# A decoder block with a product-key expert mixer: more buffers for expert rows, fewer for gathered rows, and another pacing of lookups and gathered rows beside the dense expert passes

## The chip, the cores and the metric

The kernel runs on one core of one Trainium2 chip. The metric is the device time of one execution in microseconds. Three runs of the kernel before took 1950.27, 1951.07 and 1956.48 us; the median is 1951.07 us.

## What is computed

A token block of 512 rows (plus 16 meta tokens) of width 1024 goes through an attention and gated-linear-attention mixer and then through a mixer of 16384 single-neuron experts. For the change only the second part matters, cut here to its core:

```python
s1, s2 = scores of each head's query halves against 128 keys each
v1, i1 = top_k(s1, 16);  v2, i2 = top_k(s2, 16)
sc, pos = top_k(v1[:, None] + v2[None, :], 16)          # 8 heads x 16 experts per token
eidx  = take(i1 * 128 + i2, pos);  gates = softmax(sc)
act   = gelu(einsum('nkd,nd->nk', expert_u[eidx], x))   # U
y     = einsum('nk,nkd->nd', gates * act, expert_v[eidx])  # V
```

Everything is float32; products on TensorE are made of three float32r products of a high and a low part (`mm3`).

## The kernel before, in words

The 512 tokens are four blocks of 128. For blocks 0 to 2 (`DENSE`) the mixer is dense: every one of the 128 groups of 128 experts is multiplied with all 384 tokens. The pass over U, `u_phase(i1)` for 128 values of i1, loads a 512 KB block `uf` of U on SP's queue (L960), splits it into `uh` on ScalarE (L185) and `ul` on VectorE (L186), makes 24 matmuls into a bank `pj`, and writes the gelu `ge`; the first 24 results stay in SBUF, the others go to DRAM (`Ad`) in pairs of blocks on ScalarE's queue. The pass over V, `v_operands(i1)` and `v_block`, again for 128 values, loads a 512 KB block of V into the same tiles `uf` (L1006), reads `ge` back from `Ad` (L1003, one load for two blocks), multiplies it with the gates `gt` (L1021), splits both and makes 18 matmuls of 512 columns into six accumulators. `gt` comes from a table `Gd` in DRAM, 1.5 MB for eight blocks in rows of 512 bytes, also on SP's queue (L1019), two buffers.

`Gd` is written beforehand: for each dense token block `topk` finds the experts (VectorE alone but for 32 matmuls) and `spread` turns them into gate tables by one-hot products: `B` on VectorE (L877), `Am` on GpSimd (L879), matmuls into banks `px` and `pk` (L883), a copy `st` on ScalarE (L884), 32 such pieces a block.

For token block 3 (`GATHER`) the mixer is sparse: `gathered(3)` fetches for each of its 128 choices the 128 rows of U (`u_dot`, a 512 KB indirect DMA from GpSimd's queue into `gu`, L823, and a dot product on VectorE, L830) and later the 128 rows of V (`v_sum`, the same DMA and a multiply-add into `y` on VectorE, L841): 256 gathered tiles in all, called rows below, into a ring of `GB` buffers.

What mixes these is a queue of Python generators. After each block i1 the kernel calls `look.run(4.3 * RATES[0])` while lookups and spreads are left, then `rows.run(4.3 * RATES[0])` for gathered rows beside U, and `rows.run(4.3 * RATES[1])` beside V. Each generator yields a guess of its cost in us (a lookup piece 1.4, a spread piece 1.0, a row 1.3), and `run` takes pieces until the budget is spent. The gathered rows can't start before the last spread, since their buffers take the memory of the spreads. The framework's scheduler then fixes each engine's order; every engine and every queue runs its own list in order.

Below, a **step** is one U or V block, counted by its split `ul` on VectorE: steps 0 to 127 are U, 128 to 255 are V.

Of the kernel before, what the change touches and what calls it, by code (L numbers as in the profile page):

```python
# [9 lines left out]
F32 = mybir.dt.float32  # L10
# [11 lines left out]
D = 1024  # L22
KT = 8
# [4 lines left out]
NK = 128  # L28
TK = 16
WF = 2  # L30
GB = 8

GEB = 4

# [3 lines left out]
ORDER = ("nqaylvorx", "nlvorxqay")  # L38


RATES = (0.75, 0.45)


SCHED = "f f f u1 f f t0 c1 f f f f m m"
# [24 lines left out]
def build(tc, d, out):  # L69
# [12 lines left out]
    def pool_close(key):  # L82
        stk.pop(key).__exit__(None, None, None)
# [9 lines left out]
    def pj():  # L93
        return psA.tile([128, 512], F32, name="pj", bufs=2)
# [89 lines left out]
    def hilo(hi, lo, src):  # L184
        A.activation(hi, src, AF.Copy)  # L185
        V.tensor_tensor(lo, src, hi.bitcast(F32), op=OP.subtract)  # L186

    def mm3(outp, l, r, first, last):
        (lh, ll), (rh, rl) = l, r
        T.matmul(outp, lh, rh, start=first, stop=False, skip_group_check=True)  # L190
        T.matmul(outp, lh, rl, start=False, stop=False, skip_group_check=True)  # L191
        T.matmul(outp, ll, rh, start=False, stop=last, skip_group_check=True)  # L192
# [628 lines left out]
    def gather(table, col):  # L821
        u = gb.tile([128, D], F32, name="gu", bufs=GB)
        P.indirect_dma_start(out=u, out_offset=None, in_=d[table],  # L823
                             in_offset=bass.IndirectOffsetOnAxis(ap=col, axis=0))
        return u
# [109 lines left out]
    def ring_tile(i):  # L935
        for o, n, nm in rblk:
            if i == o and ring[i] is None:
                t = pp.tile([128, n, ND * 128], F32, name=nm)
                ring[o:o + n] = [t[:, j] for j in range(n)]
                uname[o] = t  # L940
        return ring[i]

    def u_phase(i1, early=False):
        nonlocal gp
        if i1 < R:
            dst = ring_tile(i1)
        else:
            if i1 % 2 == 0:
                gp = du.tile([128, 2, ND * 128], F32, name="ge", bufs=GEB)
            dst = gp[:, i1 % 2]  # L950
        if early:
            if not uname.get("e"):
                uname["e"] = pp.tile([128, 2, KT, 128], F32R, name="oT0l"), pp.tile([128, KT, 128], F32, name="kT0")
            e, uf = uname["e"]
            uh, ul = e[:, 0], e[:, 1]
        else:
            uf = du.tile([128, KT, 128], F32, name="uf", bufs=2)
            uh = du.tile([128, KT, 128], F32R, name="uh", bufs=2)
            ul = du.tile([128, KT, 128], F32R, name="ul", bufs=2)
        nc.sync.dma_start(uf, d["expert_ut"][i1])  # L960
        hilo(uh, ul, uf)
        pu = pj()[:, :ND * 128]
        for kt in range(KT):
            mm3(pu, (uh[:, kt], ul[:, kt]), (pers["xDh"][:, kt], pers["xDl"][:, kt]), kt == 0, kt == KT - 1)
        A.activation(dst, pu, AF.Copy if early else AF.Gelu)  # L965
        if i1 >= R and i1 % 2:
            nc.scalar.dma_start(Ad[i1 // 2], gp)

    early = 0
    for st in SCHED.split():  # L970
        if st == "f":
            next(f1, None)
        elif st == "m":
            next(m1)
        elif st[0] == "c":
            next(tks[int(st[1])])
        elif st[0] == "t":
            for _ in tks[int(st[1])]:
                pass
        else:  # L980
            for _ in range(int(st[1:])):
                u_phase(early, True)
                early += 1
# [5 lines left out]
    du = ctx.enter_context(tc.tile_pool(name="dnu", bufs=1, reuse_waits="tile"))  # L989
# [5 lines left out]
    def v_operands(i1):  # L995
        nonlocal gt
        nonlocal gp
        if i1 < R:
            ge = ring_tile(i1)
        else:  # L1000
            if i1 % 2 == 0:
                gp = du.tile([128, 2, ND * 128], F32, name="ge", bufs=GEB)
                nc.sync.dma_start(gp, Ad[i1 // 2])  # L1003
            ge = gp[:, i1 % 2]
        vf = du.tile([128, D], F32, name="uf", bufs=2)
        nc.sync.dma_start(vf, d["expert_v"][i1 * 128:(i1 + 1) * 128, :])  # L1006
        if i1 == NK - 1:
            vh, vl = (gb.tile([128, D], F32R, name="gu", bufs=GB) for _ in range(2))
            w = gb.tile([128, 2, ND * 128], F32R, name="gu", bufs=GB)
            wh, wl = w[:, 0], w[:, 1]  # L1010
        else:
            vh = du.tile([128, D], F32R, name="uh", bufs=2)
            vl = du.tile([128, D], F32R, name="ul", bufs=2)
            wh = dp.tile([128, ND * 128], F32R, name="wh2", bufs=2)
            wl = dp.tile([128, ND * 128], F32R, name="wl2", bufs=2)
        hilo(vh, vl, vf)
        if i1 % IC == 0:
            gt = dp.tile([128, TB, IC, TT], F32, name="gt", bufs=2)
            nc.sync.dma_start(gt, Gd[:, :, i1:i1 + IC, :].rearrange("a p i t -> p a i t"))  # L1019
        g3 = ge.rearrange("p (a t) -> p a t", t=TT)  # L1020
        V.tensor_tensor(g3, g3, gt[:, :, i1 % IC, :], op=OP.mult)  # L1021
        hilo(wh, wl, ge)
        return wh, wl, vh, vl

    def v_block(i1, i, ops, js=(0, 1)):
        wh, wl, vh, vl = ops
        ts = slice(i * 128, (i + 1) * 128)
        for j in js:
            ds_ = slice(j * 512, (j + 1) * 512)
            mm3(acc[i][j], (wh[:, ts], wl[:, ts]), (vh[:, ds_], vl[:, ds_]), i1 == 0, i1 == NK - 1)  # L1030
# [3 lines left out]
    def gathered(blk):  # L1034

        y = gb.tile([128, D], F32, name="y")
        ys[blk] = y
        nc.sync.dma_start(y, hd[blk])
        for hh in range(NH + 1):
            if hh < NH:  # L1040
                for k in range(hh * TK, (hh + 1) * TK):
                    u_dot(blk, k)
                    yield 1.3
                weights(blk, slice(hh * TK, (hh + 1) * TK))
            if hh > 0:
                for k in range((hh - 1) * TK, hh * TK):
                    v_sum(blk, y, k)
                    yield 1.3
# [10 lines left out]
    for i1 in range(early, NK):  # L1059
        u_phase(i1)  # L1060
        if look is not None:
            look.run(4.3 * RATES[0])
            if not look.jobs or i1 == NK - 1:
                look.run(1e9)
                look = None
                pool_close("bld")
                pool_close("mid")
                gb = ctx.enter_context(tc.tile_pool(name="gat", bufs=1, reuse_waits="tile"))
                gen = gathered(3)
                rows = Queue(gen)  # L1070
        else:
            rows.run(4.3 * RATES[0])
    dp = ctx.enter_context(tc.tile_pool(name="dn", bufs=1, reuse_waits="tile"))
    pool_close("ps")
    pd = ctx.enter_context(tc.tile_pool(name="psd", bufs=1, space=PSUM, reuse_waits="tile"))
# [2 lines left out]
    for i1 in range(NK):  # L1078
        last[i1] = v_operands(i1)
        if i1 < NK - 3:  # L1080
            ops = last.pop(i1)
            for i in range(ND):
                v_block(i1, i, ops)
        rows.run(4.3 * RATES[1])
    for _ in gen:
        pass
    for i in range(ND):
        for j in range(2):
            for i1 in sorted(last):
                v_block(i1, i, last[i1], (j,))  # L1090
    gf = du.tile([128, D], F32, name="uf", bufs=2)
    nc.sync.dma_start(gf, d["gf"].to_broadcast([128, D]))
    tc.keep_in_program_order(A.preload_act_table_set(LNEXP))

# [81 lines left out]
```

## Time and profile before

| what | value |
|---|---|
| median of three runs | 1951.07 us |
| the profiled execution | 1950.29 us, of which the span from first to last instruction is 1948.5 us |
| mean granted TensorE clock | 0.941 of full speed |
| busy: TensorE, VectorE, ScalarE, GpSimd | 86%, 63%, 37%, 27% of the span |
| moved by DMA | 416.94 MB, 214 GB/s over the span |

The averages hide the stages: the DMA queues are nearly idle in one part of the program and full in another. The page's 40 slices and the table by stretches show that. Times in the trace are us from the span's start. A wait is put down to what ended it, and a chain of waits is followed back from the last instruction.

### The profile page before, as it was taken

What the parts mean: (1) busy time and instruction counts of PE and PEld (TensorE: products, weight loads), DVE (VectorE), ACT (ScalarE), POOL (GpSimd) and SP (SyncE); (2) the same over time, 40 slices, a digit from 0 to 9 for tenths busy, and PEclk for the clock granted to TensorE, in tenths of its full rate; (3) what the DMA queues carried; (4) which work ended last, traced back from release to release, by engine and by line L of the source; (5) the groups of instructions that cost most, each with busy time, mean ns of one, the idle gap of its engine ahead of it and who ended that gap; (6) DMA issues with size and microseconds to landing.
All of it is one profiled execution on the core that took longest, in us unless ns stands there. A gap on an engine that the chain in (4) does not pass through costs nothing.

```text
span 1948.5 us, 24683 instructions
## 1 busy us (share of the span) xinstructions
PE 1669.6 (86%) x9025; PEld 1457.9 (75%) x9025; DVE 1234.0 (63%) x2484; ACT 712.8 (37%) x1110; POOL 532.0 (27%) x401
## 2 busy tenths in 40 slices
PE   6999989866699999899986986688978887878995
PEld 6858989644599999899986876666766665666784
DVE  4218363894925826954856886676767766767554
ACT  5455463234134634543642222222322232222342
POOL 0020000002002602521654674443434433331000
PEclk9999999987899999999998998898999998999998
DMA  5202252420534554454689999996989988988653
GB/s 163 83 12 87 64 174 86 159 66 11 171 130 154 192 190 162 155 195 161 221 278 334 410 394 336 362 346 237 318 303 310 314 308 280 309 292 291 200 171 130
DMA packets 160682, 416.94 MB, mean 214 GB/s; under 512 B 15377, under 2 KB 64673, under 8 KB 157489
## 3 DMA queue, kind: packets, MB, share of 16 engines
q1 hardware_dynamic: 111600, 232.37, 36.6%
q0 software_dynamic: 36864, 134.23, 18.1%
q10 hardware_dynamic: 12096, 48.76, 6.3%
q8 instruction: 71, 1.16, 0.2%
q14 instruction: 51, 0.41, 0.1%
HBM read 365.48 MB, written 49.81 MB: 213 GB/s over the span
## 4 chain that ended last, share of the span: by engine, by line
PE 47%; DMA 21%; DVE 17%; issue 8%; ACT 4%; POOL 2%; SPq 0%; DVEq 0%; ACTq 0%; POOLq 0%
PE pj L190 8%; PE pj L192 8%; PE pj L191 8%; DMA uf<-expert_v 8%; DMA ge<-Ad 6%; PE acc L191 4%; PE acc L192 4%; PE acc L190 4%; DMA uf<-expert_ut 3%; DVE ul L186 3%; POOL gu L823 2%; PE pk L212 2%; DVE y L841 2%; DVE wl L186 2%; PE pk L883 1%
## 5 line engine op out<-in xcount | busy, mean ns | idle before, releaser
L186 DVE TENSOR_TENSOR ul<-uf,uh 128x1024 fp32r<-128x1024 f32 x254 | 311.3, 1226 | 329.1 <-ACT uh L185 327.3
L185 ACT ACTIVATE uh<-uf 128x1024 fp32r<-128x1024 f32 x254 | 267.9, 1055 | 530.7 <-PE pj L191 218.3
L190 PE MATMUL pj<-xDh,uh 128*128 128x384 f32 x1016 | 351.3, 346 | 53.0 <-ACT ge L965 52.3
L192 PE MATMUL pj<-xDh,ul 128*128 128x384 f32 x1016 | 347.8, 343 | 12.5 <-DVE ul L186 11.8
L191 PE MATMUL acc<-ul,wh 128*128 128x512 f32 x762 | 313.1, 411 | 44.3 <-DVE ul L186 43.9
L190 PE MATMUL acc<-uh,wh 128*128 128x512 f32 x762 | 307.9, 406 | 46.3 <-ACT uh L185 46.3
L191 PE MATMUL pj<-xDl,uh 128*128 128x384 f32 x1016 | 344.7, 339 | 0.0
L192 PE MATMUL acc<-uh,wl 128*128 128x512 f32 x762 | 307.1, 403 | 0.9 <-DVE wl L186 0.9
L879 POOL TENSOR_TENSOR Am<-ohu,ohl 128x512 f32<-128x512 f32 x96 | 154.5, 1630 | 379.7 <-PE pk L883 187.6
L823 POOL DMA_INDIRECT gu<-expert_v,idx x128 | 175.1, 1368 | 256.7 <-DVE y L841 168.5
L190 PEld LDWEIGHTS pj<-xDh,uh 128*128 128x128 f32 x1016 | 195.1, 192 | 58.3 <-ACT ge L965 57.3
L823 POOL DMA_INDIRECT gu<-expert_u,idx x128 | 175.3, 1370 | 180.4 <-DVE gu L830 86.6
L191 PEld LDWEIGHTS acc<-ul,wh 128*128 128x128 f32 x762 | 149.6, 196 | 95.0 <-DVE ul L186 63.8
L190 PEld LDWEIGHTS acc<-uh,wh 128*128 128x128 f32 x762 | 149.1, 196 | 83.8 <-ACT uh L185 51.8
L192 PEld LDWEIGHTS pj<-xDh,ul 128*128 128x128 f32 x1016 | 194.2, 191 | 20.7 <-DVE ul L186 19.2
L191 PEld LDWEIGHTS pj<-xDl,uh 128*128 128x128 f32 x1016 | 195.1, 192 | 0.0
L192 PEld LDWEIGHTS acc<-uh,wl 128*128 128x128 f32 x762 | 149.4, 196 | 32.3 <-DVE wl L186 1.6
L841 DVE SCALAR_TENSOR_TENSOR y<-gu,act,y 128x1024 f32<-128x1024 f32 x128 | 163.7, 1279 | 0.0
L830 DVE SCALAR_TENSOR_TENSOR gu<-gu,xn 128x1024 f32<-128x1024 f32 x128 | 153.9, 1219 | 11.0 <-DMA gu<-expert_u,idx 11.0
L185 ACT ACTIVATE wh<-ge 128x384 fp32r<-128x384 f32 x103 | 53.9, 523 | 260.6 <-PE acc L191 251.6
L877 DVE TENSOR_TENSOR B<-io,iT 128x512 f32<-128x512 f32 x96 | 110.5, 1178 | 15.0 <-PE px L883 11.8
L186 DVE TENSOR_TENSOR wl<-wf,wh 128x1024 fp32r<-128x1024 f32 (+1 forms) x42 | 49.7, 1186 | 88.5 <-ACT wh L185 80.7
(381 smaller groups left out, 2356.8 us busy)
## 6 DMA issues: line engine op xcount, KB each, us to landing
uf<-expert_v SPq DMA_DIRECT2D x128, 512.0 KB
uf<-expert_ut SPq DMA_DIRECT2D x127, 512.0 KB
wf<-w_in SPq DMA_DIRECT2D x48, 512.0 KB
Gd<-st ACTq DMA_DIRECT2D x24, 1024.0 KB
gt<-Gd SPq DMA_DIRECT2D x16, 1536.0 KB
Ad<-ge ACTq DMA_DIRECT2D x52, 384.0 KB
ge<-Ad SPq DMA_DIRECT2D x52, 384.0 KB
wf<-w_out SPq DMA_DIRECT2D x16, 512.0 KB
```

The source lines that it names most:

```text
L185: A.activation(hi, src, AF.Copy)
L186: V.tensor_tensor(lo, src, hi.bitcast(F32), op=OP.subtract)
L190: T.matmul(outp, lh, rh, start=first, stop=False, skip_group_check=True)
L191: T.matmul(outp, lh, rl, start=False, stop=False, skip_group_check=True)
L192: T.matmul(outp, ll, rh, start=False, stop=last, skip_group_check=True)
L212: T.matmul(o, l, r, start=st, stop=sp, skip_group_check=True)
L823: P.indirect_dma_start(out=u, out_offset=None, in_=d[table], in_offset=bass.IndirectOffsetOnAxis(ap=col, axis=0))
L830: V.scalar_tensor_tensor(u, u, 1.0, xns[blk], op0=OP.mult, op1=OP.mult, accum_out=acts[blk][:, k:k + 1]))
L841: V.scalar_tensor_tensor(y, u, acts[blk][:, k:k + 1], y, op0=OP.mult, op1=OP.add))
L877: V.tensor_tensor(B, io4, iT[:, 1, c_].unsqueeze(2).to_broadcast(sh), op=OP.is_equal)
L879: P.tensor_tensor(Am.rearrange("p t (u l) -> p t u l", l=8), ohu[:, l_].unsqueeze(3).to_broadcast([128, 4, 16, 8]), ohl[:, l_].unsqueeze(2 ...
L883: T.matmul(p[:, j * 128:(j + 1) * 128], B[:, j], Am[:, j], start=True, stop=True)
```

## The change

`uf` gets four buffers instead of two in all three places where it is made (U blocks, V blocks, and the last norm's factors), the ring of gathered rows six instead of eight, and there are three rates instead of two: 1.2 for lookups and spreads (0.75 before), 0.68 for gathered rows beside U (0.75 before), 0.45 beside V, as before.

```diff
-GB = 8
+GB = 6
+UF = 4
...
-RATES = (0.75, 0.45)
+RATES = (1.2, 0.68, 0.45)
...
-            uf = du.tile([128, KT, 128], F32, name="uf", bufs=2)
+            uf = du.tile([128, KT, 128], F32, name="uf", bufs=UF)
...
-        vf = du.tile([128, D], F32, name="uf", bufs=2)
+        vf = du.tile([128, D], F32, name="uf", bufs=UF)
...
             look.run(4.3 * RATES[0])
...
-            rows.run(4.3 * RATES[0])
+            rows.run(4.3 * RATES[1])
...
-        rows.run(4.3 * RATES[1])
+        rows.run(4.3 * RATES[2])
...
-    gf = du.tile([128, D], F32, name="uf", bufs=2)
+    gf = du.tile([128, D], F32, name="uf", bufs=UF)
```

By the built programs, the last piece of a spread stands before step 85 in the kernel before and before step 55 in the changed one. Before, steps 87 to 127 carry 107 of the 256 rows on VectorE and steps 128 to 226 the other 149; changed, steps 55 to 127 carry 170 and steps 128 to 185 the other 86, and steps 186 to 255 none. In SP's order four loads of `gt` stood among the U blocks, now five. Line numbers of the changed kernel are two higher.

VectorE within the first spread, two steps. In the kernel before (`ul` is the split of a U block, `B` a piece of a spread, `ohu` and `ohl` its one-hot tables):

```order
L186 TENSOR_TENSOR ul_5045<-uf_5043,uh_5044 128x1024
L877 TENSOR_TENSOR B_5027<-io128_80,iT_4727 128x512
L877 TENSOR_TENSOR B_5076<-io128_80,iT_4727 128x512
L865 TENSOR_TENSOR ohu_5149<-io128_80,iT_4727 128x256
L868 TENSOR_TENSOR ohl_5151<-io128_80,iT_4727 128x128
L870 TENSOR_TENSOR ohl_5151<-ohl_5151,iT_4727 128x128
L186 TENSOR_TENSOR ul_5117<-uf_5115,uh_5116 128x1024
```

In the changed one, within the second spread (`sc`, `vv` and `iu` belong to the lookup of the next block):

```order
L188 TENSOR_TENSOR ul_6067<-uf_6065,uh_6066 128x1024
L879 TENSOR_TENSOR B_5975<-io128_80,iT_5720 128x512
L879 TENSOR_TENSOR B_6018<-io128_80,iT_5720 128x512
L879 TENSOR_TENSOR B_6028<-io128_80,iT_5720 128x512
L879 TENSOR_TENSOR B_6038<-io128_80,iT_5720 128x512
L867 TENSOR_TENSOR ohu_6129<-io128_80,iT_5720 128x256
L870 TENSOR_TENSOR ohl_6131<-io128_80,iT_5720 128x128
L752 MATCH_REPLACE sc_5691<-vv_6368,sc_5691 128x128
```

Some two pieces stood between two splits, now four.

VectorE in the gathered rows beside U, before (`gu` is a row's buffer, `act3` takes its dot products):

```order
L830 SCALAR_TENSOR_TENSOR gu_9014,act3_94<-gu_9014,xn3_3900 128x1024
L186 TENSOR_TENSOR ul_9061<-uf_9059,uh_9060 128x1024
L830 SCALAR_TENSOR_TENSOR gu_9017,act3_94<-gu_9017,xn3_3900 128x1024
L830 SCALAR_TENSOR_TENSOR gu_9053,act3_94<-gu_9053,xn3_3900 128x1024
L830 SCALAR_TENSOR_TENSOR gu_9056,act3_94<-gu_9056,xn3_3900 128x1024
L186 TENSOR_TENSOR ul_9106<-uf_9104,uh_9105 128x1024
```

and changed:

```order
L832 SCALAR_TENSOR_TENSOR gu_7752,act3_94<-gu_7752,xn3_3900 128x1024
L188 TENSOR_TENSOR ul_7837<-uf_7835,uh_7836 128x1024
L832 SCALAR_TENSOR_TENSOR gu_7788,act3_94<-gu_7788,xn3_3900 128x1024
L832 SCALAR_TENSOR_TENSOR gu_7791,act3_94<-gu_7791,xn3_3900 128x1024
L188 TENSOR_TENSOR ul_7880<-uf_7878,uh_7879 128x1024
```

Rows still come two or three to a step; over the whole stretch 170 in 73 steps (2.33) in place of 107 in 41 (2.61).

SP's queue in the V blocks, around the eighth load of `gt`, before:

```order
L1003 DMA ge_11980<-Ad_75 128x768
L1019 DMA gt_12268<-Gd_73 128x24x128
L1006 DMA uf_11807<-expert_v 128x1024
L1006 DMA uf_11844<-expert_v 128x1024
L1003 DMA ge_12051<-Ad_75 128x768
```

and changed:

```order
L1005 DMA ge_12170<-Ad_75 128x768
L1021 DMA gt_12458<-Gd_73 128x24x128
L1008 DMA uf_12066<-expert_v 128x1024
L1008 DMA uf_12103<-expert_v 128x1024
L1005 DMA ge_12241<-Ad_75 128x768
```

The sequence is the same; the two `uf` behind `gt` are those of steps 171 and 172 before, of steps 173 and 174 now, while `gt` serves the same eight V blocks.

## Rows read from the trace of the kernel before

**Rows 1.** The page's 40 slices of the span (48.7 us each), busy tenths: TensorE, its granted clock in tenths, the DMA engines, and what they moved.

```profile
PE   6999989866699999899986986688978887878995
...
PEclk9999999987899999999998998898999998999998
DMA  5202252420534554454689999996989988988653
GB/s 163 83 12 87 64 174 86 159 66 11 171 130 154 192 190 162 155 195 161 221 278 334 410 394 336 362 346 237 318 303 310 314 308 280 309 292 291 200 171 130
```

**Rows 2.** Busy time by stretches: from:to and length, then busy us and instructions of TensorE, its weight loads, VectorE, ScalarE and GpSimd, the granted clock, the DMA engines' share and GB/s.

```profile
551.50:609.80 58.30, 58.30 (x342) 58.30 (x341) 17.16 (x14) 20.17 (x30) 0.00 (x0) 1.00 0.39 127
609.80:692.20 82.40, 81.45 (x552) 81.23 (x551) 59.83 (x55) 47.00 (x58) 47.07 (x27) 1.00 0.54 192
692.20:750.40 58.20, 58.20 (x347) 57.95 (x346) 17.16 (x14) 20.10 (x30) 0.00 (x0) 1.00 0.54 179
750.40:854.10 103.70, 92.06 (x594) 89.38 (x591) 97.20 (x324) 54.28 (x66) 49.10 (x32) 0.95 0.45 164
854.10:909.10 55.00, 55.00 (x319) 55.00 (x318) 15.93 (x13) 19.67 (x29) 0.00 (x0) 1.00 0.56 187
909.10:1003.70 94.60, 93.02 (x625) 92.37 (x624) 71.46 (x77) 52.41 (x64) 53.98 (x34) 1.00 0.59 207
1003.70:1263.80 260.10, 194.90 (x1010) 181.88 (x1009) 183.72 (x237) 61.65 (x91) 146.58 (x110) 0.91 0.97 366
1263.80:1803.50 539.70, 450.11 (x1798) 351.89 (x1796) 382.19 (x501) 150.33 (x203) 201.52 (x144) 0.93 0.86 301
1803.50:1917.50 114.00, 112.01 (x482) 91.48 (x483) 60.43 (x85) 45.17 (x65) 0.00 (x0) 0.99 0.55 174
1917.50:1948.50 31.00, 9.69 (x42) 7.31 (x40) 13.53 (x34) 6.90 (x21) 0.00 (x0) 0.73 0.39 135
```

**Rows 3.** The splits `ul` on VectorE in the same stretches: busy us and, in brackets, how many, which is the number of steps.

```profile
551.50:609.80 58.30, 17.16 (x14) 1.00 0.39 127
609.80:692.20 82.40, 16.80 (x13) 1.00 0.54 192
...
909.10:1003.70 94.60, 18.32 (x15) 1.00 0.59 207
1003.70:1263.80 260.10, 51.38 (x42) 0.91 0.97 366
1263.80:1803.50 539.70, 120.88 (x99) 0.93 0.86 301
1803.50:1917.50 114.00, 34.24 (x28) 0.99 0.55 174
```

**Rows 4.** The gathers' issues (L823) on GpSimd in the two stretches that hold gathered rows: busy us and how many.

```profile
1003.70:1263.80 260.10, 146.58 (x110) 0.91 0.97 366
1263.80:1803.50 539.70, 201.52 (x144) 0.93 0.86 301
```

**Rows 5.** Groups of instructions: how many, busy us and mean ns of one, idle time before them and what ended it.

```profile
L186 DVE TENSOR_TENSOR ul<-uf,uh 128x1024 fp32r<-128x1024 f32 x254 | 311.3, 1226 | 329.1 <-ACT uh L185 327.3 <-issue 1.7
L841 DVE SCALAR_TENSOR_TENSOR y<-gu,act,y 128x1024 f32<-128x1024 f32 x128 | 163.7, 1279 | 0.0
L879 POOL TENSOR_TENSOR Am<-ohu,ohl 128x512 f32<-128x512 f32 x96 | 154.5, 1630 | 379.7 <-PE pk L883 187.6 <-DVE ohl L870 148.2 <-PE px L883 28.8
L877 DVE TENSOR_TENSOR B<-io,iT 128x512 f32<-128x512 f32 x96 | 110.5, 1178 | 15.0 <-PE px L883 11.8 <-PE pk L883 3.2
```

**Rows 6.** DMA issues by line: queue, how many, KB each.

```profile
uf<-expert_v SPq DMA_DIRECT2D x128, 512.0 KB
...
gt<-Gd SPq DMA_DIRECT2D x16, 1536.0 KB
Ad<-ge ACTq DMA_DIRECT2D x52, 384.0 KB
```

**Rows 7.** SP's issues around a load of `gt` in the U blocks: start, length with the waits between, line and what.

```profile
1157.09 0.38 SPq L1019 DMA_DIRECT2D gt<-Gd  x1
1161.08 27.96 SPq L960 DMA_DIRECT2D uf<-expert_ut  x4
```

**Rows 8.** The chain of waits that ended last, at that place and at a load of `gt` in the V blocks: start, length, what.

```profile
1161.08 21.19 DMA uf<-expert_ut
...
1433.49 2.28 DMA ge<-Ad
1435.78 15.69 DMA uf<-expert_v
```

**Rows 9.** Who waited for whom in the V blocks with gathered rows (1263.8 to 1803.5): us in total, times, longest.

```profile
ACT uh L185 <- DMA uf<-expert_v: 123.2, 38, 11.5
...
DVE ge L1021 <- DMA ge<-Ad: 59.5, 25, 4.9
```

**Rows 10.** The same view over the whole span: GpSimd's waits for free row buffers, and VectorE's for rows that had not landed.

```profile
POOL gu L823 <- DVE y L841: 229.3, 111, 16.5
...
POOL gu L823 <- DVE gu L830: 166.4, 70, 15.9
...
DVE gu L830 <- DMA gu<-expert_u,idx: 11.0, 8, 8.2
```

**Rows 11.** Two more stretches, with the columns of rows 2: the last weights before the U pass, and U blocks with gathered rows between two loads of `gt`.

```profile
523.00:552.00 29.00, 26.59 (x187) 25.04 (x187) 15.95 (x32) 8.85 (x18) 0.00 (x0) 0.96 0.48 164
...
1187.00:1243.00 56.00, 51.59 (x283) 48.60 (x281) 49.41 (x64) 15.93 (x23) 39.47 (x30) 1.00 1.00 388
```

## The prediction

> **What bounds the kernel now.** The 40 slices [rows 1] come first: TensorE is full from slice 12 to 20, and the DMA engines are half idle there; from slice 21 on they are at nine or ten tenths and TensorE is not full. The table by stretches [rows 2] with the number of steps in each [rows 3] turns that into prices.
>
> Bare U (551.5 to 609.8): 14 steps in 58.3 us, TensorE busy throughout, 4.16 us a step. With a spread beside it: 82.4 us for 13 steps and 94.6 us for 15, so 28.3 and 32.2 us above bare steps; TensorE stays busy for 98 to 99% [rows 2, 3], so a piece costs about 1 us of TensorE and nothing waits. In 750.4 to 854.1, where a lookup meets a spread, VectorE bounds: busy 97.2 of 103.7 us [rows 2].
>
> U with gathered rows (1003.7 to 1263.8): 42 steps in 260.1 us, 6.2 us a step, 110 gathers issued [rows 2, 3, 4]. The DMA engines are busy 97% and move 366 GB/s; TensorE idles 65 us. This stretch is bound by DMA. In its smooth part, between two loads of `gt`, it is at 100% and 388 GB/s [rows 11]. Around a load of `gt` the SP queue shows why it is not always so: `gt` was issued at 1157.1, the next U block at 1161.1, and the chain waits 21.2 us for that block [rows 7, 8]. A load of 1.5 MB in 512-byte pieces stands ahead of it in the same queue, and two buffers of U reach no further than two steps.
>
> V with gathered rows (1263.8 to 1803.5): 99 steps in 539.7 us, 5.45 a step, 144 gathers [rows 2, 3, 4]; V alone afterwards: 28 steps in 114 us, 4.07 a step [rows 2, 3]. DMA is at 86%, and what ends last is a late block of V (123.2 us in 38 waits) or a late `ge` (59.5 us in 25) [rows 9]; the chain shows such a wait behind `gt`, 15.7 us [rows 8].
>
> So 260.1 - 42 x 4.16 = 85 us are lost beside U and 539.7 - 99 x 4.07 = 137 us beside V, all in stretches that hold gathered rows.
>
> **The change part by part.** I follow the time at which each stage ends.
>
> *Lookups and spreads at rate 1.2.* Nothing is added or removed: the same 96 pieces and three lookups, with fewer U steps between them. The last spread piece now precedes step 55 instead of 85. Thirty-one bare steps move out from ahead of the gathered rows: 1003.7 - 31 x 4.16 = 874.7 us. Four pieces in a step are more than two; would another engine bound? GpSimd needs 4 x 1.63 = 6.5 us, VectorE 1.23 + 4 x 1.18 = 5.9 us and some 1.3 for three small tables, TensorE 4.16 + 4 x 1.0 = 8.2 us [rows 2, 3, 5]. TensorE still bounds, so I take zero there, with GpSimd's 6.5 us the nearest cover. The lookup beside a spread is bound by VectorE as before, with four more pieces in it (5 us, of which TensorE's other work covers part). Before the U pass the order changes: three U blocks that stood between the last weight loads now stand behind them, and six spread pieces take their place. TensorE was busy 26.6 of 29 us there [rows 11]. Loss at most 3 x 4.16 = 12.5 us; gain by the pieces about 6 us. I add 6 us for all of this (bounds 0 and 18): the rows start at **881 us** (875 to 893) instead of 1003.7.
>
> *Rows beside U at rate 0.68.* 73 steps now carry 170 rows, with about 6 more in flight at the end. The stretch is bound by DMA, so I count bytes. A row or a U block is 0.524 MB; a pair of blocks writes 0.393 MB to `Ad`; a `gt` is 1.573 MB [rows 6]. Rows: 176 x 0.524 = 92.3 MB. U: 73 x 0.524 = 38.3. `Ad`: 73 x 0.197 = 14.4. `gt`: 5 loads, 7.9. The block `y`: 0.5. Sum 153.4 MB. At 366 GB/s, the old stretch with its stalls, that is 419 us [rows 2]; at 388 GB/s, the smooth part, 395 us [rows 11]. Four buffers of `uf` keep SP issuing for two steps longer while `gt` passes, which fills part of the idle DMA time but leaves the crawl of the 512-byte pieces. I take 412 us, nearer the lower rate (bounds 395 and 425, the latter 1.5% below 366 GB/s). The other engines fit under 5.6 us a step: VectorE 1.23 + 2.33 x 1.28 = 4.2 us and TensorE 4.16 [rows 3, 5]. U ends at 881 + 412 = **1293 us**, against 1263.8: later, because it carries 170 rows instead of 107.
>
> A rule speaks against this rate. The row shows 388 GB/s over 56 us [rows 11]. The Trainium skill, "DMA: Bandwidth & Descriptors", section "Where 436 GB/s comes from", says that transfers between HBM and SBUF are bound by the HBM side at some 358 GB/s for a core. By it the stage would take 153.4 / 0.358 = 428 us, an estimate from that page, and the sum would be 16 us higher. The trace does not agree, so I stay with its rows.
>
> *Six buffers for rows.* GpSimd waits for a free buffer for 229 and 166 us, but VectorE waited for a row in 8 cases only, 11.0 us in all [rows 10]. Rows land long before they are used; the buffers hold waiting rows. Two fewer cost nothing while that cover lasts. What it costs if it is gone is the second rival.
>
> *V with gathered rows.* Only 86 rows are left, over 58 steps, at the old density (1.48 a step, 149 in 99 before). Unchanged, such a step costs 5.45 us: 316 us. With four buffers the block of V is issued four steps ahead instead of two, some 8 us more, about half of the 15.7 us wait. The late blocks were 123.2 / 99 = 1.24 us a step [rows 9]; without any of it a step is 4.2 us. But `ge` is not moved: its load is still released by its own four buffers, and stands behind the same `uf` and `gt`, so its waits (0.6 us a step) stay [rows 9]. The bytes give a floor: 82 rows, 58 blocks of V, 21 loads of `ge` and 7 of `gt` are 92.7 MB, 253 us at 366 GB/s. I take somewhat under half of the late blocks' time as gained, 0.55 us a step: 4.9 us, **284 us** (bounds 253 and 316). Gathered rows end at 1577 us.
>
> *V alone.* 69 steps from 186 to 255 at 4.07 us: 281 us, to 1858 us. The tail from the last split is 31.0 us as before [rows 2]: a span of **1889 us**. The profiled execution took 1.8 us more than its span, so 1891 us against its 1950.29. The median of the runs, 1951.07, is 0.8 us from that, and I make no correction.
>
> By stages: 123 us sooner at the start of the rows, 152 us more beside U, 256 us less beside V with rows, 167 us more of V alone: -60 us. The gain is not that DMA does less; it is that fewer V steps share it, and that more of the program's end runs at 4.07 us.
>
> **The rivals.**
>
> *Four V buffers don't help* (chance 0.15). If `ge` behind `gt` holds VectorE anyway, V blocks land in time for nothing and a step stays at 5.45 us: 316 in place of 284, 1923 us. For it: each `ge` is used about one step after it is issued, before and now; the chain passes through `ge` just ahead of the 15.7 us [rows 8]. Against it: the late blocks are twice the late `ge` [rows 9].
>
> *Six row buffers are too few* (0.08): **slower.** In the U stretch each of 8 buffers came round in 8 x 260.1 / 110 = 18.9 us [rows 4]. If that time is latency and not waiting in the ring, 6 buffers give 0.317 rows a us, 176 rows take 555 us instead of 412, and the end comes at 2034 us. It decides from a round of 16.1 us, where the stage takes 472 us and the gain is eaten. For it: GpSimd does wait for buffers most of the time. Against it: the 11.0 us of VectorE's waits for rows [rows 10], and 8 x 56 / 30 = 14.9 us for a round in the smooth part, where VectorE was busy 49.4 of 56 us [rows 11] and rows waited for it.
>
> *Four buffers pay in full* (0.10): 395 us beside U, 255 beside V, 1845 us. For it: DMA at 100% between two `gt`. Against it: the 512-byte loads still cross the gathers' packets.
>
> *DMA is slower when it must be full for 400 us* (0.07): if it moves what the old stretch moved, 366 GB/s [rows 2], or 4% less for its fifth `gt` and longer queues, the stage takes 419 to 437 us and the end comes at 1898 to 1916 us, still faster. Against it stand the 388 GB/s of the smooth part [rows 11]. The Trainium skill's section named above, with its 358 GB/s, would put the time inside this span. That the pieces don't move as the rates say is ruled out by the order.
>
> **How the numbers follow.** The forecast, 1891 us, keeps 0.60, with 20 us on either side for its own terms. The range 1850 to 1935 takes in the first and the fourth rival and the nearer part of the third; it leaves out the second and the far end of the third, some 0.13 together. A measurement of this kernel tells about 0.3% (5.9 us) from no change. Faster by more than that takes the forecast, the first, third and fourth rival less a few mixed cases: 0.87; within it 0.05, where a weak form of the second rival meets the first; slower 0.08.
>
> **What would show it.** In the changed profile: the first gathers at 870 to 895 us; spreads with four pieces in steps of about 8.2 us and TensorE full; U ending at 1275 to 1310 us with DMA at 97% or more; V with rows at 4.6 to 5.2 us a step over 58 steps, with late V blocks well under 1.2 us a step and `ge` waits as before; then 69 steps at 4.07. The forecast is wrong if VectorE waits for rows by more than some 50 us in the U stretch (six buffers), or if the spread steps take over 9 us.

## The result and the profile after

| | before | changed |
|---|---|---|
| median of the runs on one chip | 1950.67 us (4 runs) | 1901.17 us (4 runs) |
| the profiled execution | 1950.29 us | 1903.64 us, span 1901.8 us |
| rows start | 1003.8 us | 914.9 us |
| U with rows | 260 us, 42 steps, 6.19 us each | 393.1 us, 73 steps, 5.39 us each |
| V with rows | 540 us, 99 steps, 5.45 us each | 280.4 us, 58 steps, 4.83 us each |
| V alone | 28 steps, 4.07 us each | 69 steps, 4.07 us each |

The ratio is 0.9752, interval 0.9708 to 0.9797. The forecast was 1891 us; its range holds the result.

The slices of the changed kernel, as in [rows 1] (TensorE, its granted clock, the DMA engines, GB/s):

```profile
PE   6999999867679997799788778998998889999995
...
PEclk9999999987889999899899889999999999999998
DMA  5202142430243444355999999999988997767653
GB/s 167 85 12 79 65 163 85 160 100 12 100 177 130 169 150 169 138 177 198 343 408 378 375 346 386 377 410 388 343 319 308 344 321 223 229 215 231 205 174 111
```

Slices are counted from 0; one is 47.5 us long here and 48.7 us in [rows 1]. The full DMA slices begin at slice 19 instead of 20 or 21, and they end at slice 32 instead of 36. TensorE is less full early, in slices 11, 15 and 16; slices 8 to 10 are no fuller in the kernel before.

The stretches, with the columns of [rows 2]: from the second U step to the first row, U with rows, V with rows, V alone.

```profile
559.40:914.80 355.40, 318.64 (x2016) 312.86 (x2017) 237.12 (x461) 165.22 (x202) 129.11 (x87) 0.96 0.47 164
914.80:1307.90 393.10, 324.42 (x1772) 315.62 (x1771) 301.60 (x371) 107.89 (x157) 238.65 (x173) 0.93 1.01 384
1307.90:1588.30 280.40, 248.76 (x1044) 199.02 (x1044) 217.73 (x278) 86.03 (x119) 120.51 (x81) 0.98 0.91 323
1588.30:1869.00 280.70, 277.29 (x1212) 226.46 (x1211) 151.25 (x209) 107.23 (x147) 0.00 (x0) 1.00 0.65 207
```

The splits `ul` alone in two of them, as [rows 3]: they give the number of steps.

```profile
914.80:1307.90 393.10, 89.19 (x73) 0.93 1.01 384
1307.90:1588.30 280.40, 70.76 (x58) 0.98 0.91 323
```

Beside U the DMA engines are now full for the whole stretch and move 384 GB/s, against 366 before. The V step with rows lost 0.62 of the 1.24 us that late blocks had cost.

The waits for transfers over the whole span (us in total, times, longest):

```profile
DVE ge L1023 <- DMA ge<-Ad: 114.6, 49, 5.0
...
ACT uh L187 <- DMA uf<-expert_ut: 50.0, 3, 17.5
...
DVE gu L832 <- DMA gu<-expert_u,idx: 31.2, 30, 4.7
...
DVE y L843 <- DMA gu<-expert_v,idx: 10.1, 13, 1.2
...
ACT uh L187 <- DMA uf<-expert_v: 5.0, 2, 3.9
```

Late V blocks are gone: 5.0 us in 2 waits, where [rows 9] had 123.2 in 38. Late rows are 41 us in all, where [rows 10] had 11.0, all of it for rows of U. The wait for `ge` now leads. Of its 114.6 us, 69.9 lie in V alone, where a step takes 4.07 us as before; inside V with rows it is 44.7 us in 18 waits, 0.77 us a step, against 59.5 in 25 (0.60 a step) in [rows 9].

The chain at such a place (start, length, what) shows its form:

```profile
1426.93 0.47 DVE ge L1023
1427.40 0.48 DVE wl L188
...
1427.89 6.49 DMA ge<-Ad
...
1438.25 0.48 DVE wl L188
...
1438.75 4.85 DMA ge<-Ad
```

VectorE multiplies `ge` by the gates (`ge L1023`) and splits it (`wl`), which frees the buffer. The next load then starts, and VectorE stands at the next product until it lands. What stands behind the product in VectorE's order waits with it, ready or not.

The early part of the program lost time, too. Three stretches of it, with the columns of [rows 2]: a spread, a lookup beside a spread, a spread. They hold 4, 10 and 8 steps.

```profile
620.30:656.10 35.80, 32.02 (x227) 31.12 (x226) 31.03 (x29) 21.68 (x26) 25.99 (x16) 1.00 0.51 176
703.40:810.00 106.60, 83.47 (x530) 80.84 (x528) 99.83 (x333) 49.53 (x61) 44.33 (x35) 0.90 0.42 147
843.20:914.80 71.60, 64.03 (x447) 62.24 (x446) 57.62 (x55) 41.94 (x50) 49.35 (x31) 1.00 0.56 205
```

A spread step with four pieces takes 35.8 / 4 = 8.95 us, 71.6 / 8 the same, and TensorE idles in a tenth of it. TensorE's own rows in one such step (start, length, what, and in brackets the idle time and what ended it):

```profile
630.02 1.06 PE L885 MATMUL px<-Am,B 128*128 128x128 f32 x8
...
632.19 1.13 PE L885 MATMUL pk<-Am,B 128*128 128x128 f32 x8 [0.95 <-ACT st L886]
```

and ScalarE's just before:

```profile
628.25 1.06 ACT L187 ACTIVATE uh<-uf 128x1024 fp32r<-128x1024 f32 x1 [2.77 <-PE pj L193]
629.22 0.47 ACT L967 ACTIVATE kT<-pj 128x384 f32<-128x384 f32 x1
629.59 1.08 ACT L886 ACTIVATE st<-px 128x512 f32<-128x512 f32 x1
...
631.13 1.05 ACT L886 ACTIVATE st<-pk 128x512 f32<-128x512 f32 x1 [0.47 <-PE px L885]
```

Here the fourth piece needs the bank `pk`. Its previous content is copied out by ScalarE (`st`), which does that in its own order behind the block's `uh` and the copy `kT`. TensorE waits 0.95 us for it. The copy itself began 0.47 us late, since ScalarE waited for TensorE's third piece.

That is so in the four steps of the first stretch. In the eight of the last one TensorE's wait is as long, but it is for `B` on VectorE:

```profile
855.12 1.13 PE L885 MATMUL px<-Am,B 128*128 128x128 f32 x8 [0.95 <-DVE B L879]
```

Four pieces `B` take VectorE 5.99 us in such a step, 1.5 us each where [rows 5] has a mean of 1.18, and VectorE idles only 0.94 us of the 8.95. So the bank is not the whole cause; neither wait was cured by itself.

Last, SP's issues ahead of the U pass:

```profile
528.16 15.15 SPq L201 DMA_DIRECT2D wf<-w_pq  x6
543.36 30.13 SPq L962 DMA_DIRECT2D uf<-expert_ut  x8
```

U blocks follow only when the last weights `w_pq` have been issued. The second U step's split comes at 559.5 us, in the kernel before at 527.3.

### The profile page after: what moved, and what is told of

It reads as the page before. It is cut to its first block, busy times and chain, and to the rows that moved or that the text cites. A ratio compares the mean times of both kernels' runs of the same rounds, so it can differ in the third digit from the quotient of the medians.

```text
span 1901.8 us, 24746 instructions
## 1 busy us (share of the span) xinstructions
PE 1649.2 (87%) x9025; PEld 1455.6 (77%) x9025; DVE 1238.7 (65%) x2484; ACT 710.6 (37%) x1110; POOL 533.0 (28%) x401
## 4 chain that ended last, share of the span: by engine, by line
PE 20%; DMA 15%; issue 8%; DVE 5%; POOL 4%; ACT 1%; DVEq 0%; SPq 0%; POOLq 0%; ACTq 0%
DMA ge<-Ad 7%; PE acc L193 6%; PE acc L192 6%; PE acc L194 6%; POOL gu L825 4%; DMA gu<-expert_v,idx 3%; DMA uf<-expert_ut 3%; DVE ul L188 1%; DVE y L843 1%; DVE wl L188 1%; PE pj L194 1%; PE pj L192 1%; PE pj L193 1%; DMA uf<-expert_v 1%; DVE ge L1023 1%
## 5 line engine op out<-in xcount | busy, mean ns | idle before, releaser
L193 PE MATMUL acc<-ul,wh 128*128 128x512 f32 x762 | 302.3, 397 | 33.9 <-DVE ul L188 33.7
L192 PE MATMUL acc<-uh,wh 128*128 128x512 f32 x762 | 299.0, 393 | 1.2 <-ACT uh L187 1.2
L194 PE MATMUL acc<-uh,wl 128*128 128x512 f32 x762 | 299.4, 393 | 0.0
L881 POOL TENSOR_TENSOR Am<-ohu,ohl 128x512 f32<-128x512 f32 x96 | 142.0, 1504 | 306.1 <-PE pk L885 142.6
L825 POOL DMA_INDIRECT gu<-expert_u,idx x128 | 181.3, 1416 | 150.2 <-DVE gu L832 91.3
L825 POOL DMA_INDIRECT gu<-expert_v,idx x128 | 180.0, 1406 | 148.7 <-DVE y L843 112.0
L193 PEld LDWEIGHTS acc<-ul,wh 128*128 128x128 f32 x762 | 144.4, 190 | 75.1 <-DVE ul L188 45.3
L194 PEld LDWEIGHTS acc<-uh,wl 128*128 128x128 f32 x762 | 144.6, 190 | 29.5
L879 DVE TENSOR_TENSOR B<-io,iT 128x512 f32<-128x512 f32 x96 | 117.7, 1265 | 26.1 <-PE pk L885 14.5
L1023 DVE TENSOR_TENSOR ge<-ge,gt 128x384 f32<-128x384 f32 x104 | 54.8, 555 | 114.7 <-DMA ge<-Ad 114.6
## 6 DMA issues: line engine op xcount, KB each, us to landing
gt<-Gd SPq DMA_DIRECT2D x16, 1536.0 KB, 13.8
```

Source lines behind the costliest of these rows:

```text
L825: P.indirect_dma_start(out=u, out_offset=None, in_=d[table], in_offset=bass.IndirectOffsetOnAxis(ap=col, axis=0))
L879: V.tensor_tensor(B, io4, iT[:, 1, c_].unsqueeze(2).to_broadcast(sh), op=OP.is_equal)
L881: P.tensor_tensor(Am.rearrange("p t (u l) -> p t u l", l=8), ohu[:, l_].unsqueeze(3).to_broadcast([128, 4, 16, 8]), ohl[:, l_].unsqueeze(2 ...
```

## The experiments

Medians stand against runs of the kernel before in the same comparison (1946 to 1950 us); a ratio's 95% interval is in brackets. Stage numbers come from one profiled execution each, which lies up to 7 us from the median of its runs.

**The change in halves.** First the rates alone, on the kernel before.

```diff
-RATES = (0.75, 0.45)
+RATES = (1.2, 0.68, 0.45)
```

> The new rates alone, with two buffers for U and V rows and eight for gathered rows as before. Theory (the late blocks behind gt are what four buffers cure): gathered rows start near 915 us as in the changed kernel, the U stretch runs at the old 366 GB/s (419 us), the V stretch at the old 5.45 us a step (58 steps, 316 us), then 281 and 33 us: span about 1964 us, no gain or 1% slower than before. Rival (the gain comes from moving rows ahead into the U pass): 30 to 50 us faster than before, about 1905 to 1920.

1935.5 us, 0.9936 [0.9904, 0.9968]: between the two theories, so neither. Rows start at 900.2 us, U with rows costs 5.76 us a step at 361 GB/s, V with rows 5.01, V alone 4.22. The rates alone pay a quarter of the gain.

Then the buffers alone, with the old rates.

```diff
-GB = 8
+GB = 6
+UF = 4
...
-RATES = (0.75, 0.45)
+RATES = (0.75, 0.75, 0.45)
...
+... name="uf", bufs=UF)
```

> The buffers alone (four for U and V rows, six for gathered rows), with the rates before, 0.75 for lookups and for rows beside U. Theory: rows start at 1004 us as before, 95 MB in the U stretch at 390 GB/s (244 us), 99 V steps with rows at 4.83 us (478 us), 114 and 31 us: about 1871 us, faster than the whole change. Rival (moving the rows is what gains): little, 1930 us or more.

1919.2 us, 0.9859 [0.983, 0.9888]: again between the two theories, 1871 us and 1930 or more. Rows start at 1014.1, U with rows 5.80 us a step (382 GB/s), V with rows 5.14. The buffers are the larger half; the two ratios multiply to 0.980, and both together gave 0.9752 [0.9708, 0.9797].

The change with only two V buffers:

```diff
-UF = 4
+UF = 2
```

> The changed kernel with two buffers for U and V rows again, gathered rows still six. Theory: like the rates alone, about 1964 us, since two fewer buffers for gathered rows cost little (10 us at most). Rival (six are too few): 20 us or more above the rates alone, and VectorE waits for rows by more than 60 us.

1933.7 us, 0.9919 [0.9887, 0.9951]: like the rates alone, as the theory said, though both lie some 30 us below the 1964 that it gave. U 5.72 us a step (361 GB/s), V with rows 5.17. Its waits for blocks, over the whole span:

```profile
ACT uh L187 <- DMA uf<-expert_ut: 234.2, 55, 17.7
...
ACT uh L187 <- DMA uf<-expert_v: 104.3, 39, 11.1
```

With two more buffers these 338 us are 55. Since this kernel (six row buffers) and the rates alone (eight) agree within their intervals, going from eight to six costs nothing that can be told, with two `uf`; with four it was not run. Four row buffers:

```diff
-GB = 6
+GB = 4
```

> The changed kernel with four buffers for gathered rows instead of six. In the changed kernel VectorE waited 41 us for rows, against 11 before. Theory: the ring now runs short, those waits double or triple, and the end comes 20 to 50 us later, about 1920 to 1950 us. Rival (rows wait in the ring anyway): within 8 us of the changed kernel's 1901.

1926.9 us, 0.9887 [0.9845, 0.9928]: some 26 us lost, all beside U (5.78 us a step), as the theory said. VectorE's waits for rows go from 41 to 114 us:

```profile
DVE gu L832 <- DMA gu<-expert_u,idx: 76.7, 53, 6.5
...
DVE y L843 <- DMA gu<-expert_v,idx: 37.4, 38, 2.4
```

So the ring can be too small: with four buffers it is.

**Why the rows start late.** By the addresses of the built program, which no trace shows, the pool of U blocks and `ge` ended below the last weights' staging tiles with two `uf`, and with four it reaches into them. So no U block could be loaded before those weights had been used. If so, `ge` in a pool of its own gives the time back:

```diff
+    dg = ctx.enter_context(tc.tile_pool(name="dge", bufs=1, reuse_waits="tile"))
...
-                gp = du.tile([128, 2, ND * 128], F32, name="ge", bufs=GEB)
+                gp = dg.tile([128, 2, ND * 128], F32, name="ge", bufs=GEB)
```

> The changed kernel, with the buffers ge taken out of the pool of uf, uh and ul into a pool of their own behind it. Theory: with four uf the one pool reaches into the memory of the weight buffers wf and oT1h, so no U block may start before the last weights are used (second split at 559 us against 527 with two uf); a pool without ge ends ahead of them, U starts at 530 us or sooner, rows start 13 to 15 us earlier (about 900 us), about 1886 us in all. Rival (the late start comes of the denser lookups): rows start at 915 us as in the changed kernel, 1901 us.

1879.3 us, 0.9646 [0.9592, 0.9699]. The second split comes at 493.6, rows start at 892.4 instead of 914.9, and every later stage is as in the changed kernel (5.36, 4.88, 4.04 us a step). It gives back more than four `uf` had taken: rows start 9 us sooner than in the changed kernel with two `uf` (901.3). SP's issues now mix U blocks with the weights:

```profile
492.14 0.86 SPq L962 DMA_DIRECT2D uf<-expert_ut  x2
495.82 5.39 SPq L201 DMA_DIRECT2D wf<-w_out  x2
...
512.67 4.03 SPq L201 DMA_DIRECT2D wf<-w_pq  x2
524.67 1.53 SPq L962 DMA_DIRECT2D uf<-expert_ut  x2
```

The rate of the lookups, lowered:

```diff
-RATES = (1.2, 0.68, 0.45)
+RATES = (0.95, 0.68, 0.45)
```

> The changed kernel with lookups and spreads at 0.95 instead of 1.2. Theory (four pieces in a step run out of banks px and pk, since ScalarE's copy of the first piece stands behind its split and gelu: 8.95 us a step instead of 7.8): three pieces in a step take about 6.9 us with TensorE full; rows start some 12 steps later, so more rows are left beside V; the two nearly cancel, 1895 to 1910 us. Rival (bursts cost nothing): spread steps keep the price of 1.2 us a piece, 1910 us or more.

1905.5 us, 0.9791 [0.975, 0.9833], no difference from the change. A step with three pieces takes 6.87 us, with four 8.92; with three TensorE has no such wait, which does not tell the bank from VectorE's pieces. What the cheaper spreads gave (rows start at 948.4, 14 steps later) was lost again in V: 79 steps with rows at 5.06 us.

**What late blocks wait behind.** With two buffers, `gt` moved off SP's queue:

```diff
-            nc.sync.dma_start(gt, Gd[:, :, i1:i1 + IC, :].rearrange("a p i t -> p a i t"))
+            nc.scalar.dma_start(gt, Gd[:, :, i1:i1 + IC, :].rearrange("a p i t -> p a i t"))
```

> The changed kernel with two uf again (the same as the third run) and gt loaded on ScalarE's queue instead of SP's. Theory (U and V blocks are late because gt stands ahead of them in one queue): ScalarE's wait for U and V blocks, 234 and 104 us with two uf, falls by half or more, the V stretch with rows goes from 5.17 to 4.9 us a step or less, the U stretch from 418 to about 400 us, the end comes 20 to 35 us sooner, about 1900 to 1915 us. Rival (two buffers are too few beside any gather, gt or not): less than 8 us gained against the third run's 1934.

1896.1 us, 0.9724 [0.9673, 0.9775]: 38 us below the same kernel with `gt` on SP, and level with four buffers. U runs at 380 GB/s. The time came out as said, the waits did not: their totals were to fall by half or more and fell by a quarter and by a twentieth. What fell by about half are the longest ones:

```profile
ACT uh L187 <- DMA uf<-expert_ut: 177.2, 52, 7.5
...
ACT uh L187 <- DMA uf<-expert_v: 98.7, 43, 5.9
```

So four buffers and a queue of its own for `gt` both cure the long waits, in which blocks stand behind a 1.5 MB load (13.8 us from issue to landing). That the two kernels are level does not make them alike: here 276 us of short waits for blocks stay and those for `ge` are 68.1 us in all, with four buffers it is 55 and 114.6.

**What waits for `ge`.** The product by the gates is kept at its place in the program, so that the scheduler doesn't pull it ahead:

```diff
-        V.tensor_tensor(g3, g3, gt[:, :, i1 % IC, :], op=OP.mult)
+        tc.keep_in_program_order(V.tensor_tensor(g3, g3, gt[:, :, i1 % IC, :], op=OP.mult))
```

> The changed kernel with the product of ge and gt held in program order on VectorE, so that it stands at its own step, seven steps behind the load of ge instead of one. Theory (what is left beside V is VectorE standing at a ge that has not landed, 115 us in 49 waits): those waits fall under 15 us, the V stretch with rows goes from 4.83 to about 4.3 us a step, 25 to 35 us less, about 1870 us. Rival (the product is now late for the matmuls of its own step, or the bytes bound it): V steps stay at 4.8 us, or those without rows rise over 4.07; 1900 us or more.

1862.1 us, 0.9562 [0.952, 0.9604]. The waits for `ge` are gone: none is left. Its two stretches with rows, columns as [rows 2]:

```profile
914.90:1278.10 363.20, 321.01 (x1761) 312.47 (x1760) 290.11 (x344) 106.26 (x154) 242.38 (x172) 0.97 1.02 400
1278.10:1547.90 269.80, 246.52 (x1049) 193.22 (x1049) 228.64 (x296) 89.80 (x119) 120.48 (x83) 1.00 0.99 353
```

Of the 39 us, 30 came beside U and only 11 beside V, where the theory had expected all of it (4.3 us a step; it is 4.65). The product had run ahead into the U blocks, and had pulled loads of `gt` with it. SP's issues beside U in the changed kernel:

```profile
943.87 111.21 SPq L962 DMA_DIRECT2D uf<-expert_ut  x23
1059.69 0.38 SPq L1021 DMA_DIRECT2D gt<-Gd  x1
1060.82 36.30 SPq L962 DMA_DIRECT2D uf<-expert_ut  x7
1098.46 0.38 SPq L1021 DMA_DIRECT2D gt<-Gd  x1
...
1162.01 0.38 SPq L1021 DMA_DIRECT2D gt<-Gd  x1
```

and in the pinned one:

```profile
930.85 1.26 SPq L1021 DMA_DIRECT2D gt<-Gd  x1
935.21 322.47 SPq L962 DMA_DIRECT2D uf<-expert_ut  x66
```

Five loads among the U blocks (two more at 917.4 and 930.1 us) became two. In V with rows, which now moves 95 MB in place of 91, DMA is at 99%. So the late `ge` seems to have hidden a bound by DMA, some 11 us further down.

The same edit on the kernel before:

> The kernel before with one edit: the product of ge and gt in program order on VectorE. Theory (late blocks behind gt and the wait for ge are two separate losses): VectorE's 75 us of waits for ge vanish and V steps with rows come to about 5.1 us, but late U and V blocks stay near their 284 us with two uf: 25 to 40 us sooner than before, 1908 to 1923 us. Rival (the wait for ge was the whole loss, and four uf only help beside it): 70 us or more sooner, 1880 us or less.

1945.5 us, 0.9986 [0.9956, 1.0016]: nothing. The theory fell, and so did the rival. The waits for `ge` are gone here, too, and beside U it did gain (5.60 us a step, 387 GB/s), but V with rows went to 5.53 us a step over 101 steps, with late blocks as before:

```profile
ACT uh L185 <- DMA uf<-expert_ut: 149.7, 35, 18.5
...
ACT uh L185 <- DMA uf<-expert_v: 122.9, 39, 10.9
```

Two loads of `gt` left the U blocks for V here. That with two `uf` they delay V blocks instead, which four would bridge, is inferred: inside V with rows the waits for blocks did not grow (111.4 us in 36, 123.2 in 38 in [rows 9]). But the 59.5 us for `ge` that vanished there bought nothing, so they had been covered by other waits. The same edit is worth nothing on one and 39 us on the other.

**Together.** Own pool for `ge` and the pinned product, on the changed kernel:

> The changed kernel with both cures: ge in a pool of its own and the product of ge and gt in program order. Theory (the two act at different places, the start of U and the rows beside U and V): they add, 22 us and 39 us below the changed kernel, about 1840 us. Rival (an earlier start only moves rows into a stretch that is bound by bytes): 1850 us or more.

1840.8 us, 0.9439 [0.9411, 0.9467]. Start 892.1, U 4.99, V with rows 4.68: the two gains add up.

The same with `gt` on ScalarE's queue as well:

> Both cures, and gt on ScalarE's queue with four uf. Theory (four uf already hide the load of gt, so that the queue no longer matters): within 8 us of the run with both cures, about 1840 us. Rival (U and V blocks are still held up behind gt): 10 us or more sooner, 1830 us or less.

1857.5 us, 0.9543 [0.9519, 0.9566]: 17 us slower, which neither theory held. U and V with rows are within 5 us of the kernel without it, but V alone rose from 4.05 to 4.26 us a step. Every eighth step there takes 6.2 us in place of 4.1, seven steps and 15 us in all. ScalarE at one of them:

```profile
1619.04 0.37 ACTq L1022 DMA_DIRECT2D gt<-Gd  x1
...
1624.30 1.06 ACT L187 ACTIVATE uh<-uf 128x1024 fp32r<-128x1024 f32 x1 [3.02 <-PE acc L194]
1625.27 0.51 ACT L187 ACTIVATE wh<-ge 128x384 fp32r<-128x384 f32 x1
```

Behind the issue of `gt`, the split `wh` of a block stands after the next block's `uh`; in the other steps it stands before it. TensorE waits 1.61 us for this `wh`. That the issue brought about this order is inferred from the place. ScalarE also waited at an issue before `uh` four times, 23.8 us in all, but beside U: the longest, 15.6 us, follows a store to `Ad` that stands behind two loads of `gt` in ScalarE's queue.

And with the old rates:

```diff
-RATES = (1.2, 0.68, 0.45)
+RATES = (0.75, 0.75, 0.45)
```

> Both cures with the rates of the kernel before (0.75, 0.75, 0.45). Theory (a V step with rows costs some 0.6 us more than one without even when nothing is late, since DMA is nearly full there, so taking 41 V steps out of the rows' stretch pays): 15 to 30 us above the run with both cures, 1855 to 1870 us. Rival (with the waits gone the rows' place is indifferent): within 8 us of it, about 1840 us.

1833.3 us, 0.9404 [0.9382, 0.9426]: the fastest of all, level with the new rates within the intervals. Its two stretches with rows:

```profile
993.30:1226.30 233.00, 192.17 (x1022) 184.36 (x1021) 177.15 (x217) 61.01 (x88) 150.85 (x109) 0.93 1.01 389
1226.30:1698.20 471.90, 427.54 (x1810) 334.97 (x1809) 396.51 (x523) 156.22 (x207) 210.12 (x145) 1.00 0.98 354
```

The theory (15 to 30 us slower) fell and the rival held. The balance of the profiled executions shows why. New rates cost at the start: rows begin at 892.1, where the old ones less 31 bare steps give 993.3 - 31 x 4.16 = 864.3, so 28 us. They save later what rows cost above bare steps: 58 us beside U and 65 beside V with old rates (233.0 - 42 x 4.16; 471.9 - 101 x 4.03), 61 and 36 with new ones, so 26 us. Where blocks and `ge` still come late the second number is larger: without the two cures, four `uf` and old rates lose 69 and 106 us, the changed kernel 89 and 44, so 42 us saved for 30.

## Why the prediction was right or wrong

**The start of the rows** is the step that failed: 881 us forecast (875 to 893), 914.9 measured. Three terms were mis-sized.

The order ahead of the U pass was put at 6 us, for three U blocks that move behind the last weight loads. The real cause was the larger pool, not the rates: with the rates alone rows start at 900.2, with two `uf` in the changed kernel at 901.3, with `ge` in its own pool at 892.4. Four `uf` cost about 14 us there (10 with the old rates).

The pieces were priced at zero under TensorE's 8.2 us a step, with GpSimd's 6.5 us the nearest cover. They take 8.95 us: 12 such steps x 0.75 us are 9 us. TensorE idles 0.95 us in each, by the rows for a bank in four of them and for VectorE's `B` in eight. VectorE was the nearer cover: it needs 8.0 us and not 5.9 and some 1.3, since pieces beside GpSimd's `Am` take longer than the mean. The kernel before already held such a step, from 639.74 us on, and it took 8.92 us:

```profile
640.88 5.99 DVE L877 TENSOR_TENSOR B<-io,iT 128x512 f32<-128x512 f32 x4
...
648.66 1.23 DVE L186 TENSOR_TENSOR ul<-uf,uh 128x1024 fp32r<-128x1024 f32 x1 [0.92 <-ACT uh L185]
```

The third term is the 31 steps. The lookup beside the second spread is bound by VectorE, as forecast, but it lasts as long as before (106.6 us against 103.7) and covers 10 U steps, not 13. Those three steps come afterwards, 12 to 15 us: the prediction moved 31 steps out as if each had cost 4.16 us of its own, while some of them had been free in VectorE's shadow.

**Rows beside U**: 412 us forecast, 393.1 measured, just under the lower bound of 395. The bytes were right (384 GB/s x 393 us = 151 MB, 153.4 counted); the rate was taken too low, 372 against 384 GB/s. Four buffers filled the gaps around `gt` and not half of them: two-buffer kernels run at 361 GB/s in the same stretch. The Trainium skill, "DMA: Bandwidth & Descriptors", "Where 436 GB/s comes from", with some 358 GB/s for one core's HBM side, is not borne out here: 384 GB/s lasted 393 us, and 400 GB/s lasted 363 us in the pinned kernel.

**Six row buffers** cost nothing that the runs can tell, as forecast; the rival's mechanism exists, and costs 26 us with four. VectorE's waits for rows did grow, from 11 to 41 us.

**V with rows**: 4.9 us a step forecast, 4.83 measured. "Somewhat under half of the late blocks' time" was half. Late blocks went entirely; waits for `ge` grew from 0.60 to 0.77 us a step, the first rival's mechanism. That is as much as is left above 4.07 us, but not the price of these waits: on the pinned kernel they are gone, and a step still takes 4.65 us, with DMA at 99%.

**V alone** was exact, 4.07 us over 69 steps. The tail took 32.8 us in place of 31.0 because another split is now the last: that of step 255 came last before, that of step 254 does now. From step 254's split on it is 32.9 us before and 32.8 now.

Together, +34 us at the start, -19 beside U, -4 beside V and +2 at the end make the 13 us between the forecast and the span. The direction stood on the right wait. The reason given at the end, that "fewer V steps share it", holds only in part: it is true while a V step with rows pays for late blocks and late `ge`, and it is worth nothing once these are cured, as the old rates show on the cured kernel.

## What to carry to other kernels

A prefetch has to reach past the longest transfer that stands ahead of it in its queue; more buffers or another queue cure the same wait, and two waits that cover one another show their worth only when both are gone. When a pool grows, look at which tiles of the neighbouring stage its addresses now touch, since it delays that stage by what those tiles' last use allows. When steps are moved out of a stretch that another engine bounds, they were free there and cost their full price elsewhere.

## What was not expected of the hardware

- The DMA engines held 384 GB/s for 393 us and 400 GB/s for 363 us with gathers, blocks and stores mixed; the slices of the changed kernel show no falling off over the length of the stretch (408 GB/s in slice 20, 410 and 388 in 26 and 27).
- VectorE's piece `B` has two lengths in both kernels. With none of GpSimd's `Am` beside it, it took 0.66 to 0.69 us; over 1.5 us it took 51 times of 96 before and 60 times in the changed kernel, each time beside an `Am`. Burst or not, the long one is as long: 3.04 us for two in one step before, 5.99 us for four. The mean of 1178 ns in [rows 5] and of 1265 ns now mixes the two. Nothing was tried on it.
- With `gt` on ScalarE's queue, ScalarE's issues of stores to `Ad` behind it took up to 15.5 us in the run with both cures and up to 12.9 us in the one with two `uf`; with `gt` on SP's queue none took over 3 us in the kernel before or in the run with both cures.
- The granted clock in V with rows rose as the waits went: 0.93 in [rows 2], 0.98 changed, 1.00 (the 2.4 GHz level throughout) pinned, with fewer gaps of TensorE each time. What of the gain is the clock's was not tried apart.
